# Expert weights as unconverted float32 in two column halves of TensorE, with four smaller moves ahead of them

## The chip, the cores and the metric

The kernel runs on 1 core of one Trainium2 chip. The metric is the device time of one execution in microseconds; lower is better. The engines are TensorE (PE, with its weight loads PEld), VectorE (DVE), ScalarE (ACT), GpSimd (POOL) and SyncE (SP), which here only issues DMAs.

## What is computed

One layer of a streaming encoder on 256 tokens of 1024 features, all in float32: three token mixers on the same input, gates, an output projection, a LayerNorm, then a mixture of 16 experts and a second LayerNorm. Cut to what matters (the routing takes one group of four experts for each token, and the best two inside it):

```python
proj = x @ w_in + b_in                        # 1024 -> 9216 columns
a = a_val * sigmoid(a_gate)                   # mixer A
a = causal_depthwise_conv(a, conv_a_w) + conv_a_b        # 31 taps
a = silu(layer_norm(a, ln_a_g, ln_a_b))
y_a = a @ w_a_out
y_b, y_c = ...                                # short convolution, pooling
mix = (g[0] * y_a + g[1] * y_b + g[2] * y_c) @ w_o + b_o
x = layer_norm(DEEPNORM_ALPHA * x + mix, ln1_g, ln1_b)
for e in range(16):                           # grouped_moe
    h = silu(x @ w_exp_gate[e]) * (x @ w_exp_up[e])      # 1024 -> 512
    y = y + combine[:, e:e + 1] * (h @ w_exp_down[e])    # 512 -> 1024
out = layer_norm(DEEPNORM_ALPHA * x + y, ln2_g, ln2_b)
```

The matrices are 152 MB in float32, each read once.

## The kernel before

**Chunks and slots.** The weights lie in memory as 145 chunks of 1 MB, 128 partitions by 2048 float32: 49 for the mixers (list `MIX`) and 96 for the experts (`EXP`), six for each expert `e`: two halves of the gate matrix (`EG`), two of the up matrix (`EU`), two of the down matrix (`ED`). `give` (L139) hands freed buffers back and issues the next chunk's load on SP whenever one of the slots of 1 MB is free, so that the loads run ahead of the work as far as the slots reach; `hold` keeps some slots back for other uses.

**Two parts for each weight.** A weight isn't multiplied as it is. ACT copies it into a rounded form, fp32r (`hi`, L163), and DVE or POOL forms the remainder (`lo`, L173); both lie in slots of their own (`H` and `L` in the rows, or other slots' names that were reused). The activations have two such parts too. A product is then three matmuls in fp32r in the mixers (L306 for chunk 0, L315 for the others, L518 for the last ones).

**Experts.** Each expert has 64 places for tokens (CAP). A gather (L836 for the first group of four experts, L944 for the others) brings the tokens' features into `XG`, transposed, the two parts side by side: a stationary tile of 128 columns, 64 with the rounded parts and 64 with the remainders. So `mm` (L980) needs two matmuls of 512 columns for each block of 128 features, one against `H` and one against `L`: 8 to a chunk, 32 for gate and up of one expert. The eviction `ev_gu` (L987, L989) adds the upper 64 rows onto the lower. `hidden` (L997) transposes the two results back, in eight blocks of 64 columns, and forms the hidden activations. For the down matrix, 80 of the 96 chunks of the experts being converted and 16 not, one half of `ED` is taken by `mm` again, and the other by `mm_native` (L1032) in plain float32 with a stationary tile of 64 columns; such a matmul stands in the trace as two instructions, each of them 512 columns. Then `scatter` (L1023, L1026) adds the expert's output, weighted, into four banks of PSUM (`acc`) that all experts share. A small matmul (L965) makes the matrices that scatter needs.

**What sets the order.** In the mixers a scheduler orders the engines' queues; `at(j, f)` ties a step to the work of chunk `j`, and `convert(j + 2)` runs two chunks ahead of the matmuls. The LayerNorm of mixer A hangs on one number, `LNA` = 34: its sums are matmuls with ones (L449 for the mean, L467 for the variance), with the squares added up by one reduction on DVE (L462) between them, and four blocks of swish for each of two chunks from `LNA + 4` on; the blocks' remainders are formed on POOL (L268). From the last mixer chunks on the order is the one that is written down (`tc.manual_schedule`), on each engine by itself. The transition between mixers and experts holds the first LayerNorm of the layer (`add1`, L642; `x1a`, L682), the logits and the softmax (L677), the choice of experts (`select`), and the comparison `places` (L820) whose result `ps` the gathers need; the conversion of the first three chunks of the experts is woven into it. The second LayerNorm (L1196 to L1220) and the stores end the kernel.

## Time and profile before

| | us |
|---|---|
| median of 3 runs | 612.66 (610.72 to 613.81) |
| profiled execution | 614.9 |
| its span in the trace | 613.1 |
| span up to the experts' first matmul | 317.3 |
| experts' stage up to the end of its last matmul | 281.5 |
| what is left to the end of the span | 14.3 |
| mean granted clock of TensorE | 0.979 of full speed |

The profiled execution is 1.8 us longer than its span, and 2.2 us longer than the median. In the rows below, L12 is line 12 of the kernel; `x` is a count of instructions; a buffer's number is left out of its name, and `128*64` is a TensorE tile of 128 rows and 64 columns. In brackets stands how long an engine was idle just ahead of the instruction, and what ended that.

### The profile page before, as it was taken

What the parts mean: (1) busy time and instruction counts of PE and PEld (TensorE: products, weight loads), DVE (VectorE), ACT (ScalarE), POOL (GpSimd) and SP (SyncE); (2) the same over time, 40 slices, a digit from 0 to 9 for tenths busy, and PEclk for the clock granted to TensorE, in tenths of its full rate; (3) what the DMA queues carried; (4) which work ended last, traced back from release to release, by engine and by line L of the source; (5) the groups of instructions that cost most, each with busy time, mean ns of one, the idle gap of its engine ahead of it and who ended that gap; (6) DMA issues with size and microseconds to landing.
All of it is one profiled execution on the core that took longest, in us unless ns stands there. A gap on an engine that the chain in (4) does not pass through costs nothing. (4 is left out here: it accounts for less than half of the span.)

```text
span 613.1 us, 9493 instructions
## 1 busy us (share of the span) xinstructions
PE 581.2 (95%) x3554; PEld 481.7 (79%) x3554; DVE 545.1 (89%) x862; ACT 373.8 (61%) x536; POOL 194.3 (32%) x150
## 2 busy tenths in 40 slices
PE   7999999999999998899999998999999999999990
PEld 5999999999999998798878466666566667666650
DVE  4899999999996578876889699899999999999985
ACT  5643544446643456745247496888678886888851
POOL 2876899987689420500000022000000000000003
PEclk9999999999999998899989997999999999999997
DMA  8985545455557645566479784899989998998102
GB/s 302 422 338 192 170 175 196 149 206 185 177 196 266 210 149 211 214 233 249 159 277 387 285 340 150 332 382 385 399 320 366 390 408 309 373 386 328 68 1 73
DMA packets 24084, 158.77 MB, mean 259 GB/s; under 512 B 2784, under 2 KB 3040, under 8 KB 5472
## 3 DMA queue, kind: packets, MB, share of 16 engines
q1 hardware_dynamic: 24032, 158.10, 68.4%
q8 instruction: 30, 0.49, 0.3%
q14 instruction: 22, 0.18, 0.1%
HBM read 157.04 MB, written 1.05 MB: 258 GB/s over the span
## 5 line engine op out<-in xcount | busy, mean ns | idle before, releaser
L315 PE MATMUL pj<-XH,H 128*128 128x256 f32 x560 | 138.7, 285 | 0.0
L315 PE MATMUL pj<-XL,H 128*128 128x256 f32 x560 | 138.3, 284 | 0.0
L163 ACT ACTIVATE H<-R 128x1024 fp32r<-128x1024 f32 (+1 forms) x74 | 72.2, 1027 | 67.2 <-issue 30.0
L315 PEld LDWEIGHTS pj<-XH,H 128*128 128x128 f32 x560 | 108.3, 193 | 0.1
L315 PEld LDWEIGHTS pj<-XL,H 128*128 128x128 f32 x560 | 108.3, 193 | 0.1
L337 DVE SCALAR_TENSOR_TENSOR z<-UP,par,z 128x256 f32<-128x256 f32 x232 | 98.8, 480 | 0.7
L173 POOL TENSOR_TENSOR L<-R,H 128x1024 fp32r<-128x1024 f32 (+2 forms) x50 | 88.0, 1783 | 21.2 <-ACT H L163 21.2
L320 PE MATMUL pj<-XH,L 128*128 128x256 f32 x560 | 78.6, 283 | 0.0
L1199 POOL TENSOR_TENSOR sm<-sm,mhalf 128x1 f32<-128x1 f32 x2 | 1.1, 551 | 228.3 <-DVE sm L1198 228.3
L173 DVE TENSOR_TENSOR L<-R,H 128x768 fp32r<-128x768 f32 (+2 forms) x46 | 62.7, 1378 | 11.5 <-ACT H L163 11.5
L320 PEld LDWEIGHTS pj<-XH,L 128*128 128x128 f32 x560 | 72.2, 192 | 0.0
L163 ACT ACTIVATE H<-S 128x1024 fp32r<-128x1024 f32 x30 | 30.1, 1050 | 29.2 <-issue 16.6
L173 POOL TENSOR_TENSOR L<-S,H 128x1024 fp32r<-128x1024 f32 (+1 forms) x20 | 36.6, 1855 | 1.1 <-ACT H L163 1.1
L987 ACT ACTIVATE t2k<-pj 64x512 f32<-64x512 f32 x32 | 19.1, 596 | 23.7 <-PE pj L980 21.5
L173 DVE TENSOR_TENSOR L<-S,H 128x768 fp32r<-128x768 f32 (+1 forms) x16 | 24.1, 1519 | 5.5 <-ACT H L163 5.4
L989 DVE TENSOR_TENSOR t2k<-pj,t2k 64x512 f32<-64x512 f32 x32 | 21.6, 676 | 3.8 <-ACT t2k L987 3.6
L268 POOL TENSOR_TENSOR R<-UP,YL 128x512 fp32r<-128x512 f32 x4 | 7.4, 1858 | 54.4 <-ACT YL L267 54.4
L1026 PEld LDWEIGHTS z<-t2k,pt 128*128 128x128 f32 x60 | 10.2, 188 | 11.2 <-ACT hs L1010 7.3
L1026 PE MATMUL z<-t2k,pt 128*128 128x512 f32 x60 | 17.7, 416 | 0.0
L944 PEld LDWEIGHTS pj<-ps,YL 128*128 128x128 f32 x48 | 8.8, 206 | 10.8 <-DVE ps L820 3.9
L268 POOL TENSOR_TENSOR AL<-t2k,AH 128x256 fp32r<-128x256 f32 x8 | 9.0, 1136 | 25.7 <-ACT AH L267 25.7
L944 PE MATMUL pj<-ps,YL 128*128 128x256 f32 x48 | 11.9, 321 | 5.2 <-DVE ps L820 4.7
(491 smaller groups left out, 1429.5 us busy)
## 6 DMA issues: line engine op xcount, KB each, us to landing
R<-w SPq DMA_DIRECT2D x51, 1024.0 KB, 5.0
S<-w SPq DMA_DIRECT2D x25, 1024.0 KB, 5.2
L<-w SPq DMA_DIRECT2D x11, 1024.0 KB, 7.4
H<-w SPq DMA_DIRECT2D x11, 1024.0 KB, 7.1
AC<-w SPq DMA_DIRECT2D x6, 1024.0 KB, 6.1
PL<-w SPq DMA_DIRECT2D x6, 1024.0 KB, 7.7
M<-w SPq DMA_DIRECT2D x6, 1024.0 KB, 7.8
XH<-w SPq DMA_DIRECT2D x6, 1024.0 KB, 7.9
```

Source lines behind the costliest of these rows:

```text
L163: S.activation(HI[j][:, o], raw[j][:, o], AF.Copy)
L173: eng.tensor_tensor(LO[j][:, o], raw[j][:, o], HI[j][:, o].bitcast(F32), op=OP.subtract)
L268: eng.tensor_tensor(dl, src, dh.bitcast(F32), op=OP.subtract)
L315: PE.matmul(p[:, c], h[:, o:o + 128], m[:, k0 + k], start=(n == 0), stop=False)
L320: PE.matmul(p[:, c], l[:, o:o + 128], ah[:, k0 + k], start=False, stop=(n == 3 * nk))
L337: V.scalar_tensor_tensor(AC[:, i] if k == TAPS - 1 else ca, src, wk, ca, op0=OP.mult, op1=OP.add)
L944: PE.matmul(p[:, n], xs[:, t, (4 * b + k) * 128:(4 * b + k + 1) * 128], PS[:, t, :, 0], start=(t == 0), stop=(t == 1))
L987: S.activation(t, p[64:], AF.Copy)
L989: V.tensor_tensor(GU[e, n], p[:64], t, op=OP.add)
L1026: PE.matmul(acc[t, b], PTs[e][:, t], YV[e, b][n], start=False, stop=(e == NE - 1 and n == 1))
L1199: G.tensor_tensor(mv[:, 2:3], mv[:, 1:2], mhalf, op=OP.pow)
```

## The change

It has five parts.

1. **Experts.** No chunk of an expert is converted. A weight chunk as it was loaded is the moving operand of a float32 matmul, and the stationary tile is 64 columns of unsplit tokens. `gate_up(e)` issues for each of eight blocks of 128 features two such matmuls, one with the gate's weights into the rows 0 to 63 of a PSUM bank and one with the up weights into the rows 64 to 127: the two stand in the two halves of TensorE's columns. `down(e)` does the same with the two halves of `ED`, four times two. There is one eviction of 128 rows on ACT, four transposes of 128 columns instead of eight of 64, and a scatter of eight matmuls for each expert, each with 64 rows of the contraction, in the two halves of the rows. The slots that held parts now hold chunks: 20 of them circulate, against some that were half as many chunks with their two parts. The expert's chunks come in the order gate, up, gate, up. The last two chunks of all, not the last one, are loaded in pieces of 512, and the last expert's `down`, its scatter and its statistics go in halves of 256 columns. The normalization at the end uses a PSUM bank between its two DVE steps, and each part is stored as soon as it is there.
2. **Chunk 0.** Its weights are laid out by feature blocks, its pieces and those of x are loaded in turn, and its matmuls go by pairs of feature blocks into two PSUM banks.
3. **LayerNorm of mixer A.** `LNA` is 31. The reduction of the squares is three additions instead, the matmul for the variance has one chunk more between itself and them, swish goes three blocks to a chunk, and its remainders are formed on DVE instead of POOL.
4. **Last mixer chunks.** For the last four of them the eviction of the chunk before (`done`) is put ahead of the conversion for the chunk after next.
5. **Transition.** The conversions of the experts' first three chunks are gone from it; the writing of a quarter of the LayerNorm (`x1a(1, 1)` and `x1b(1, 1)`, L682 and L686) goes behind `select` and `places`; matmuls whose result isn't used (`warm_up`) are 8 instead of 16; and the first gather's eviction is two copies, one on ACT and one on DVE.

The core of the diff (the loop over the experts, evictions and names that changed alike are left out):

```diff
-    def mm(p, lhs, j, first, last, mid=None):
-        h, l = HI[j], LO[j]
-        for n, ws in enumerate((h, l)):
-            if n and mid:
-                mid()
-            for k in range(4):
-                PE.matmul(p, lhs(k), ws[:, 512 * k:512 * k + 512],
-                          start=(first and n == 0 and k == 0), stop=(last and n == 1 and k == 3))
-        used(j)
+    def gate_up(e):
+        p = bank("pj", (128, 512))
+        for k in range(KT):
+            js = [INDEX[kind, e, k // 4] for kind in ("EG", "EU")]
+            for n, j in enumerate(js):
+                PE.matmul(p[64 * n:64 * n + 64], XG[e // 4][:, k, e % 4], raw[j][:, 512 * (k % 4):512 * (k % 4) + 512],
+                          start=(k == 0), stop=(k == KT - 1))
+            if k % 4 == 3:
+                for j in js:
+                    used(j)
+        g = GU[e] = t2k([128, 512])
+        S.activation(g, p, AF.Copy)
...
     def hidden(e):
-        p = bank("pj", (128, 2, 4, 64))
-        for n in range(2):
-            for k in range(4):
-                PE.transpose(p[:, n, k], GU[e, n][:, 128 * k:128 * k + 128], ident[:64, :64])
-        HS[e] = HSB
+        p = bank("pj", (128, 4, 2, 64))
+        for k in range(4):
+            PE.transpose(p[:, k], GU[e][:, 128 * k:128 * k + 128], ident)
...
+    def down(e, p, a=0, b=512):
+        js = [INDEX["ED", e, n] for n in range(2)]
+        for k in range(4):
+            for n, j in enumerate(js):
+                PE.matmul(p[64 * n:64 * n + 64], HF[e][:, k], raw[j][:, 512 * k + a:512 * k + b], start=(k == 0), stop=(k == 3))
+        if b == 512:
+            for j in js:
+                used(j)
...
-    def scatter(e, b):
+    def scatter(e, a=0, b=512):
         for t in range(2):
-            if b and e < NE - 1 or e == 0:
-                PE.matmul(acc[t, b], PTs[e][:, t], YV[e, b], start=False, stop=False)
-            else:
+            for i, y in enumerate(YV[e]):
                 for n in range(2):
-                    PE.matmul(acc[t, b], PTs[e][:, t], YV[e, b][n], start=False, stop=(e == NE - 1 and n == 1))
+                    r = slice(64 * n, 64 * n + 64)
+                    PE.matmul(acc[t, n][:, a:b], PTs[e][r, t], y[r, a:b], start=False,
+                              stop=(e == NE - 1 and i == 1), skip_group_check=(a > 0))
...
+    for e in range(NE):
+        while e // 2 not in ready:
+            some()
+        gate_up(e)
...
+        if e > 1:
+            scatter(e - 2)
...
+        last = e == NE - 1
+        if last:
+            hidden(e)
+        if e:
             p = bank("pj", (128, 512))
-            block(lambda j: mm(p, tokens(e, 0), j, True, False), before=last)
+            down(e - 1, p)
+            ev_down(e - 1, p)
+        if not last:
+            hidden(e)
...
             j = nxt[0]
             tags[j] = free.pop(-1 if dynamic[0] else 0)
             raw[j] = slot(tags[j], [128, 2048])
-            n = 512 if j == len(CHUNKS) - 1 else 2048
+            n = 512 if j >= len(CHUNKS) - 2 else 2048
             for i in range(0, 2048, n):
...
         h, l = HI[j], LO[j]
-            for c in range(js):
-                for b in range(2):
-                    for n, (ws, m) in enumerate(((h, ah), (h, al), (l, ah))):
-                        for k in range(4 * b, 4 * b + 4):
-                            o = (c * nk + k) * 128
-                            PE.matmul(p[:, c], ws[:, o:o + 128], m[:, k], start=(b == n == 0 and k == 0),
-                                      stop=(b == 1 and n == 2 and k == 7))
+            pp = [p[:, 0], bank()[:, 0]]
+            for b in range(4):
+                for n, (ws, m) in enumerate(((h, ah), (h, al), (l, ah))):
+                    for k in (2 * b, 2 * b + 1):
+                        for c in range(js):
+                            o = (k * js + c) * 128
+                            PE.matmul(pp[c], ws[:, o:o + 128], m[:, k], start=(b == n == 0 and k == 0),
+                                      stop=(b == 3 and n == 2 and k == 7))
...
-            V.tensor_reduce(sv, sq.rearrange("p i t -> p t i"), axis=AX.X, op=OP.add)
+            V.tensor_tensor(sq[:, :4], sq[:, :4], sq[:, 4:], op=OP.add)
+            V.tensor_tensor(sq[:, :2], sq[:, :2], sq[:, 2:4], op=OP.add)
+            V.tensor_tensor(sv, sq[:, 0], sq[:, 1], op=OP.add)
...
-            halves(A["h"][:, i], A["l"][:, i], z, G)
+            halves(A["h"][:, i], A["l"][:, i], z, V)
         at(j, center)
         at(j + 1, squares)
-        at(j + 1, var, True)
-        at(j + 2, rstd)
+        at(j + 2, var, True)
+        at(j + 3, rstd)
         for i in range(KT):
-            at(j + 2 + i // 4, lambda i=i: swish(i), True)
+            at(j + 3 + i // 3, lambda i=i: swish(i), True)
...
-    LNA = 34
+    LNA = 31
...
+        late = j > NM - 5
+        if done and late:
+            done()
+            done = None
         if j + 2 < NM:
             convert(j + 2, CUT if j < LNA else 0)
...
+                if a:
+                    V.tensor_copy(o, p[:, a:a + 2])
+                else:
+                    S.activation(o, p[:, a:a + 2], AF.Copy)
...
     x1a(0, 0)
     x1a(0, 1)
-    lo(C1, V, 0, 1024)
     logits(0, 0)
...
-    x1a(1, 1)
-    x1b(1, 0)
+    residual2(0, 0)
+    residual2(0, 1)
     u1 = shift1(1)
     softmax1(1, u1)
-    x1b(1, 1)
+    x1b(1, 0)
     S.activation(dummy, ex[1][:, :1], AF.Sigmoid)
-    warm_up(16)
+    warm_up(8)
     weave(best2(1), best_group(1))
     select(1)
+    x1a(1, 1)
     place1(1)
     warm_up(8)
     places(0, 1, 0, 2)
-    lo(C2, V, 0, 512)
+    x1b(1, 1)
...
-            V.scalar_tensor_tensor(u, z, mv[:, :1], g, op0=OP.subtract, op1=OP.mult)
-            V.scalar_tensor_tensor(u, u, mv[:, 2:3], c, op0=OP.mult, op1=OP.add)
-    def store(t, a, b, o):
-        nc.sync.dma_start(out[t * 128:t * 128 + 128, a:b], o[:, t, a:b])
+            v = bank("pj", (128, b - a))
+            V.scalar_tensor_tensor(v, z, mv[:, :1], g, op0=OP.subtract, op1=OP.mult)
+            V.scalar_tensor_tensor(u, v, mv[:, 2:3], c, op0=OP.mult, op1=OP.add)
```

In the rows below, a name with numbers is one use of a buffer, and line numbers are each kernel's own (L965 of after is `gate_up`, L988 `down`, L976 the transposes, L1007 the scatter).

On PE, the experts' steady work before: one expert's converted down half (against `hs`), the transposes (against `ident`), the native down half of the expert before (against `ssum`), the scatter (`z` is one bank of `acc`), and the next expert's gate.

```order
L980 MATMUL pj_4921<-H_647_4883,hs 128x512 x4
L980 MATMUL pj_4921<-M_4885,hs 128x512 x4
L997 MATMUL pj_4932<-ident,t2k_4881 128x64 x4
L997 MATMUL pj_4932<-ident,t2k_4913 128x64 x4
L1032 MATMUL pj_4958<-S_571_4572,ssum_4757 64x512 x4
L1026 MATMUL z_3628<-t2k_4943,pt_4720 128x512
L1026 MATMUL z_3628<-t2k_4944,pt_4720 128x512
L1026 MATMUL z_3626<-t2k_4943,pt_4720 128x512
L1026 MATMUL z_3626<-t2k_4944,pt_4720 128x512
L980 MATMUL pj_4967<-XL_4915,R_626_4776 128x512 x4
L980 MATMUL pj_4967<-S_655_4917,R_626_4776 128x512 x4
```

And on PE after, at the like place: the end of `down` of one expert, the transposes of the next, gate and up of the one after, in turn, and the beginning of a scatter, whose rows name two banks in turn.

```order
L988 MATMUL pj_4148<-R_413_3875,ssum_4085 64x512
L988 MATMUL pj_4148<-S_422_3902,ssum_4085 64x512
L976 MATMUL pj_4165<-ident,t2k_4124 128x128 x4
L965 MATMUL pj_4175<-AH_3904,XL_3934 64x512
L965 MATMUL pj_4175<-UP_3930,XL_3934 64x512
L965 MATMUL pj_4175<-AH_3904,XL_3934 64x512
L965 MATMUL pj_4175<-UP_3930,XL_3934 64x512
...
L965 MATMUL pj_4175<-PL_3954,XL_3934 64x512
L1007 MATMUL z_3620<-t2k_4161,pt_3889 128x512
L1007 MATMUL z_3621<-t2k_4161,pt_3889 128x512
L1007 MATMUL z_3620<-t2k_4162,pt_3889 128x512
L1007 MATMUL z_3621<-t2k_4162,pt_3889 128x512
```

The 8 rows of L980 for gate and up of one expert, of four matmuls each, are 16 single ones that alternate between two weight buffers.

On DVE, in the transition before, from the last evictions of the mixers (L642) to the second half's softmax (L677); L173 is the conversion of an expert's chunk, L682 half of the LayerNorm's writing, L820 `places`.

```order
L173 TENSOR_TENSOR H_334_3536<-R_286_3121,AH_3474 128x512 x2
L642 TENSOR_TENSOR UP_3107<-z_3280,UP_3107 128x256
...
L648 BN_STATS sm_3595<-UP_3107 128x6
L764 TENSOR_TENSOR sm_3652<-pj_3650,sm_3592 128x16
L653 BN_AGGR sm_3662<-sm_3595 128x2
L654 TENSOR_SCALAR sm_3662<-sm_3662 128x1
L682 SCALAR_TENSOR_TENSOR UP_3107<-UP_3107,sm_3662,PH_3111 128x512
L820 TENSOR_TENSOR ps<-sm_3652,slotn 128x256
L682 SCALAR_TENSOR_TENSOR UP_3107<-UP_3107,sm_3662,PH_3111 128x512
L686 SCALAR_TENSOR_TENSOR UP_3107<-UP_3107,sm_3663,PH_3111 128x512
L677 SCALAR_TENSOR_TENSOR sm_3692<-rs,sm_3662,pj_3659 128x16
```

After, at the same place.

```order
L648 BN_STATS sm_3587<-UP_3048 128x6 x2
L642 TENSOR_TENSOR UP_3048<-z_3285,UP_3048 128x256
L648 BN_STATS sm_3587<-UP_3048 128x6
L642 TENSOR_TENSOR UP_3048<-z_3285,UP_3048 128x256
L648 BN_STATS sm_3587<-UP_3048 128x6
L764 TENSOR_TENSOR sm_3644<-pj_3642,sm_3584 128x16
L653 BN_AGGR sm_3654<-sm_3587 128x2
L654 TENSOR_SCALAR sm_3654<-sm_3654 128x1
L682 SCALAR_TENSOR_TENSOR UP_3048<-UP_3048,sm_3654,PH_3052 128x512
L818 TENSOR_TENSOR ps<-sm_3644,slotn 128x256
L677 SCALAR_TENSOR_TENSOR sm_3683<-rs,sm_3654,pj_3651 128x16
```

L173 is gone from ahead of the second L642, and the second L682 stands further behind, after L677.

On DVE, around the LayerNorm of mixer A before: the square sums (L462) and the conversions (L173) beside them; L457 subtracts the mean.

```order
L173 TENSOR_TENSOR L_223_2608<-R_189_2129,H_222_2606 128x1024 x2
L173 TENSOR_TENSOR L_228_2669<-R_194_2199,H_227_2667 128x1024 x2
L173 TENSOR_TENSOR L_235_2732<-R_199_2272,H_234_2730 128x1024 x2
L457 TENSOR_TENSOR AC_170<-AC_170,t2k_2741 128x1024 x2
L443 TENSOR_TENSOR t2k_2804<-pj_2747,t2k_2675 128x512
L173 TENSOR_TENSOR L_241_2798<-R_204_2344,H_240_2796 128x1024 x2
L462 TENSOR_REDUCE t2k_2808<-PH_2729 128x256
L173 TENSOR_TENSOR L_248_2863<-S_209_2414,H_247_2861 128x1024
```

After: L459 to L461 are the three additions.

```order
L168 TENSOR_TENSOR L_214_2486<-S_181_1987,H_213_2484 128x1024 x2
L168 TENSOR_TENSOR L_221_2549<-R_185_2056,H_220_2547 128x1024 x2
L454 TENSOR_TENSOR AC_170<-AC_170,t2k_2558 128x1024 x2
L440 TENSOR_TENSOR t2k_2621<-pj_2564,t2k_2492 128x512
L168 TENSOR_TENSOR L_227_2615<-R_190_2130,H_226_2613 128x1024 x2
L459 TENSOR_TENSOR PH_2546<-PH_2546 128x1024
L460 TENSOR_TENSOR PH_2546<-PH_2546 128x512
L461 TENSOR_TENSOR t2k_2625<-PH_2546 128x256
L168 TENSOR_TENSOR L_233_2680<-R_195_2200,H_232_2678 128x1024 x2
```

The order of the steps stays, and the reduction is three instructions. On PE, the variance's matmul now has the matmuls of three chunks between itself and those for the mean, where it had two, and both stand three chunks and two chunks earlier.

## Rows read from the trace of the kernel before

**Rows 1.** The page's first part: busy us, share of the span and instructions of each engine.
```profile
PE 581.2 (95%) x3554; PEld 481.7 (79%) x3554; DVE 545.1 (89%) x862; ACT 373.8 (61%) x536; POOL 194.3 (32%) x150
```

**Rows 2.** Windows of 20 us: length, busy PE, PEld, DVE, ACT, POOL; granted clock; DMA share; GB/s.
```profile
20.00:40.00 20.00, 20.00 (x169) 20.00 (x168) 18.60 (x27) 10.49 (x13) 17.82 (x11) 1.00 1.02 415
220.00:240.00 20.00, 17.84 (x135) 17.46 (x134) 18.66 (x15) 9.34 (x12) 3.83 (x2) 0.91 0.60 211
240.00:260.00 20.00, 17.96 (x132) 17.10 (x130) 17.62 (x25) 16.34 (x30) 7.55 (x6) 0.91 0.48 168
360.00:380.00 20.00, 16.81 (x63) 11.22 (x63) 19.30 (x24) 13.82 (x23) 7.36 (x4) 0.83 0.67 264
480.00:500.00 20.00, 20.00 (x87) 13.95 (x86) 19.72 (x23) 15.86 (x22) 0.00 (x0) 1.00 0.99 388
```

**Rows 3.** The chain that ended last, inside the experts: start us, us, what.
```profile
476.37 3.72 PE pj L980 x16
480.09 0.46 PE z L1023 x2
...
484.45 2.10 PE pj L980 x8
486.55 0.64 PE pj L997 x8
487.19 3.58 PE pj L1032 x8
490.77 1.14 PE z L1026 x4
```

**Rows 4.** Timeline of PE: the experts' first and last matmuls; start us, us, instruction.
```profile
317.30 1.61 PE L980 MATMUL pj<-H,YH 128*128 128x512 f32 x4
...
597.72 1.09 PE L1026 MATMUL z<-t2k,pt 128*128 128x512 f32 x4
```

**Rows 5.** The waits, grouped: engine, line <- releaser: us, count, longest.
```profile
PE pj L944 <- DVE ps L820: 4.7, 5, 2.8
```

**Rows 6.** Timeline of PE and PEld at a plain float32 down half of 64 columns.
```profile
555.13 0.14 PEld L1032 LDWEIGHTS pj<-L,ssum 128*64 128x64 f32 x1 [0.29 <-issue]
555.56 0.14 PEld L1032 LDWEIGHTS pj<-L,ssum 128*64 128x64 f32 x1 [0.29 <-issue]
...
557.70 0.59 PE L1032 MATMUL pj<-L,ssum 128*64 128x512 f32 x1
558.23 1.21 PE L1026 MATMUL z<-t2k,pt 128*128 128x512 f32 x4
```

**Rows 7.** Groups by line and shape: ACT's conversions into one kind of slot.
```profile
L163 ACT ACTIVATE H<-R 128x1024 fp32r<-128x1024 f32 x70 | 70.0, 1050 | 65.4 <-issue 30.0 <-POOL L L173 22.0 <-PE pj L315 6.5
```

**Rows 8.** Timeline of DVE and PE around the LayerNorm of mixer A.
```profile
228.14 3.74 DVE L462 TENSOR_REDUCE t2k<-PH 128x256 f32<-128x2048 f32 x1
...
231.94 1.22 PE L467 MATMUL pj<-t2k,ones 128*128 128x256 f32 x2 [2.16 <-DVE t2k L462]
...
253.69 0.51 PE L315 MATMUL pj<-AH,H 128*128 128x256 f32 x2 [0.81 <-ACT AH L267]
255.41 0.51 PE L315 MATMUL pj<-AL,H 128*128 128x256 f32 x2 [1.22 <-POOL AL L268]
```

**Rows 9.** Timeline of DVE in the transition from the mixers to the experts.
```profile
305.38 1.28 DVE L173 TENSOR_TENSOR H<-R,AH 128x512 fp32r<-128x512 f32 x2
306.58 0.42 DVE L642 TENSOR_TENSOR UP<-z,UP 128x256 f32<-128x256 f32 x1
...
310.96 0.23 DVE L677 SCALAR_TENSOR_TENSOR sm<-rs,sm,pj 128x16 f32<-128x16 f32 x1
```

**Rows 10.** Timeline of PE at chunk 0 and at a late mixer chunk.
```profile
8.29 0.80 PE L306 MATMUL pj<-XH,H 128*128 128x256 f32 x2 [2.30 <-ACT XH L267]
...
288.92 0.73 PE L518 MATMUL z<-XH,YH 128*128 128x512 f32 x2 [0.60 <-ACT YH L267]
```

**Rows 11.** Timeline of DVE: the last step of the last LayerNorm.
```profile
606.69 0.42 DVE L1209 TENSOR_TENSOR M<-M,H 128x256 f32<-128x256 f32 x1
```

## What I predicted, and how it is worked out

> **What bounds the kernel now.** I read the busy times first: PE is busy for 581.2 of 613.1 us [rows 1], so time goes only where PE has less to do or waits less. Then the windows of 20 us, to see where it isn't full: in the first chunks and in the experts it is busy for 20.00 of 20 at clock 1.00, in the middle of the mixers there are two windows of 17.84 and 17.96 at 0.91, and one of 16.81 at 0.83 early in the experts [rows 2]. Then the chain that ended last: in the experts its pieces are PE's matmuls, end to end, and a steady expert takes 476.37 to 491.91, that is 15.54 us [rows 3]. So the experts' stage, from 317.30 to 597.72 + 1.09 = 598.81 [rows 4], 281.5 us, is a sum of matmuls. The waits come last [rows 5]: they show what could be had beside the matmuls.
>
> **Experts: what goes.** A piece of 16 matmuls of L980 takes 3.72 us [rows 3], 0.2325 each; there are 640, 40 to an expert: 148.8. The native halves: 16 of 3.58 = 57.3. Transposes: 16 of 0.64 = 10.2. Scatters: 16 of 0.46 and 15 of 1.14 [rows 3] = 24.5, and about 1.7 for the last expert's, an estimate from four of the 0.46's halves at float32's double time. Together 242.5 of 281.5. The 39.0 that remain are gathers, residual sums, small matmuls for the scatter, and waits. Their counts stay. Of the waits, 4.7 us are the gathers', for the comparison on DVE [rows 5]; it is now queued a block sooner, on an engine that loses the conversions. With the clock's dip beside it (0.83 for 20 us is 3.4 us lost [rows 2], which began with those waits) I take 5 of some 8 off: 34 stay; none or all of it is 39 or 31.
>
> **Experts: what comes.** A float32 matmul against 64 columns is two instructions, and a native half has 8 of them in 3.58 us [rows 3], 0.4475 each, so 0.895 for a matmul. Now gate and up are 16 such matmuls and down 8, each in one half of the columns, the partner right behind it in the other half. If partners run side by side, a pair costs what one does: 12 x 0.895 = 10.74 for an expert, 171.8 for 16. If not, 343.7. No row before has two matmuls in different halves of the columns; the two ends are this term's bounds. I take the first. What speaks for it: a float32 instruction of 512 columns takes 0.4475 and one of fp32r 0.2325 [rows 3], each with 512 x 4 bytes to a row, so two float32 streams at once read 2 x 512 x 4 bytes in 0.4475 us, a rate only 4% above that of one fp32r stream now.
>
> Transposes are four in place of eight; I take 0.5 of the 0.64 us (0.32 to 0.64 are the bounds): 8.0. The scatter is eight matmuls of 512 columns, in two halves of the rows: at 1.14 / 4 = 0.285 a pair [rows 3] 1.14 for an expert, 18.2; one after the other it is twice that, 36.5. Sum added: 171.8 + 8.0 + 18.2 = 198. The stage becomes 34 + 198 = 232, **-49.5**. Evictions: one ACT copy of 512 columns follows `gate_up`, and the transposes come only after `down` of the expert before, 3.6 us later; `down` needs the hidden activations only after the next `gate_up`, 7.2 us later. With the conversions gone (one piece of 1024 columns is 1.05 us on ACT [rows 7]) neither ACT nor DVE is near PE.
>
> **Loads.** What the experts need, 96 chunks, PE would now use up at 14.5 us for six. 22 are issued before the first expert frees a slot, 74 remain. At 415 GB/s, or at 388 in the experts [rows 2], a chunk of 1.05 MB takes 2.53 or 2.70 us: 187 or 200 us, under the 232. Loads decide only under 74 x 1.05 / 230 = 336 GB/s. That is why I cost them at nothing; the cover is 30 us.
>
> **Mixers.** The variance matmul waited 2.16 us for a reduction of 3.74 us, and the product after the LayerNorm 0.81 for ACT's part and 1.22 for POOL's [rows 8]: 4.2 together. The two windows at 0.91 lose 1.8 us each [rows 2], 3.6; they lie right at the waits. With one more block of cover (about 5 us of matmuls), the additions in place of the reduction, and the remainders on DVE, I expect the waits gone and half of the clock's loss: **-6**, bounds -3.8 (clock stays) and -7.8 (all). If the wait is not gone it is DVE's, whose queue now holds the remainders behind conversions.
>
> Chunk 0: PE waits 2.30 us for ACT's part of x [rows 10]; pieces in turn and pairs of features let it start with a quarter of both. PE then is bound by the pieces' arrival: **-1**, between +0.5 and -2.5. Evictions ahead of the conversions: a wait of 0.60 [rows 10], **-0.3**, 0 to -0.6. Transition: the conversion of 1.28 us stands right ahead of the last additions on DVE [rows 9], on the path PE waits for: 1.3; the step of LayerNorm's writing ahead of the softmax 1.2 (of the 310.96 - 306.58 = 4.4 between them); the first gather's evictions 0.3: **-2.8**, bounds -1.2 and -3.5. End: DVE's last step ends at 606.69 + 0.42 [rows 11]; POOL takes a part of it and a store follows each piece: **-0.5**, 0 to -1.5. Together -10.6.
>
> **Sum.** -49.5 - 10.6 = -60.1 on the profiled execution of 614.9: 554.8. That execution stands 2.2 over the median of 612.66, so the forecast is **552.6 us**. The small terms' bounds add up to about -4.5 and -16; with the 31 to 39, full overlap spans 543 to 564.
>
> **Rivals.** *Halves one after the other.* Then 171.8 us more: 552.6 + 171.8 = 724, and 743 if the scatter's halves do so too. That is slower by 18%. The mechanism is in the pair: the second matmul of 0.895 begins when the first ends. Break-even: the whole saving of 60.1 is gone when 35% of 171.8 isn't had, thus when a pair takes over 1.21 us instead of 0.895 (192 x 0.313 = 60.1). For it: no row shows an overlap. Against it: the bytes above, and that half the columns stand idle in L1032.
>
> *Loads of weights in the open.* A load of 64 columns takes 0.14 us, and follows the one before at 0.43 us [rows 6], so in one half it is hidden under the matmul. If the four loads of a pair were all in the open, 192 x 4 x 0.14 = 107.5 us more: 660. The Trainium skill, "TensorE: Matmul & The Clock Gate", Part 3, in its passage on packing small matmuls, speaks for this: it says that a load overlaps a matmul of another row group, and both halves here use all rows. The rows above speak against it: L1032's loads lie under matmuls of the same rows.
>
> *Overlap in part.* Each eighth of the second matmul's 0.895 that doesn't overlap is 192 x 0.112 = 21.5 us: 574 at one eighth, 596 at a quarter. For it: the streams ask a little more than one does now; against: no row shows two of them. The same passage of the Trainium skill gives three column tiles 2.38 times the speed of one, 0.79 of the full gain; at that the pair would be 0.895 / 0.79 = 1.13, an estimate from that page, and no run here shows it.
>
> *Loads bind.* At 300 GB/s the 74 chunks take 259 us: 28 more, 580. For it: 264 GB/s in a window of the experts [rows 2]; against: that window was slot-bound, with DMA share 0.67, and 0.99 shows 388.
>
> *Switches of the tile shape.* From the native half to the scatter PE's rows go 557.70 to 558.23, 0.53 where 0.43 is usual, and four scatter matmuls take 1.14 instead of 4 x 0.2325 = 0.93 [rows 3, 6]: some 0.3 us for such a change, which the block prices above contain. After has five to an expert where before had three: 16 x 2 x 0.3 = 10 us if none of it is in these prices: 562, inside the range. The Trainium skill, "TensorEngine Tiling (Array Packing)", Key Properties, says that a change of tiling mode drains TensorE; it agrees.
>
> **How the numbers follow.** Full overlap (540 to 565): 0.62. In part (565 to 600): 0.15. One after the other (about 724 to 743): 0.12. Loads in the open (about 660): 0.05. Bound by DMA (about 580): 0.04. Something unseen, to either side: 0.02. The range takes the first, second and fifth, 536 to 600: 0.81. Within 0.5% is about what a measurement can tell from no change; between 600 and 660 lies little, so 0.02 for the same; faster 0.82, slower 0.16.
>
> **What would show it.** `gate_up`: 16 program matmuls in some 7.2 us, `down` 3.6, a steady expert about 14.5 us where it was 15.54; records of two halves that overlap. PE still full in the experts, DMA share under 1 there, no conversions on ACT and DVE, the stage 232 us long. In the mixers: the waits of 2.16, 0.81 and 1.22 gone and the clock nearer 1.00; the experts' first matmul at about 307 instead of 317.3. It is wrong if a pair takes over 1.0 us, or if PE waits for chunks.

## The result

| | before | after |
|---|---|---|
| median, us | 612.95 (610.72 to 613.81) | 542.53 (542.26 to 543.10) |
| profiled execution | 614.9 | 543.1 |
| span | 613.1 | 541.3 |
| span up to the experts' first matmul | 317.3 | 306.0 |
| experts' stage | 281.5 | 220.9 |
| what is left | 14.3 | 14.5 |

The changed kernel takes 0.886 of the time, interval 0.883 to 0.888. The forecast was 552.6, its range 536 to 600: direction and place are right, and 10 us more were gained than forecast, nearly all of them in the experts' stage. The measured time lies just under the 543 to 564 us that the forecast's own bounds gave for full overlap; it is inside the stated range by the slack that was left below them.

The busy times after, as in [rows 1]:

```profile
PE 520.9 (96%) x3538; PEld 382.9 (71%) x3538; DVE 317.1 (59%) x626; ACT 191.3 (35%) x301; POOL 169.2 (31%) x134
```

PE is still what bounds the kernel; VectorE went from 89% to 59%. The windows of 20 us that [rows 2] show, with the same columns:

```profile
20.00:40.00 20.00, 20.00 (x169) 20.00 (x169) 19.57 (x30) 11.37 (x14) 19.02 (x11) 1.00 1.02 419
...
220.00:240.00 20.00, 20.00 (x169) 20.00 (x168) 18.43 (x26) 13.47 (x23) 3.02 (x2) 1.00 0.46 158
240.00:260.00 20.00, 20.00 (x162) 19.69 (x161) 17.40 (x30) 12.32 (x19) 0.00 (x0) 1.00 0.89 336
...
480.00:500.00 20.00, 20.00 (x100) 7.37 (x98) 3.34 (x8) 3.18 (x7) 0.00 (x0) 1.00 1.01 421
```

In the mixers PE is full at clock 1.00 where it was at 17.84, 17.96 and 0.91. In the experts VectorE and ScalarE are nearly idle, and the loads run at a DMA share of 1.01 and 421 GB/s, where the forecast went by the 388 of the window that it showed.

The chain that ended last, in one expert (start us, us, what), to be read beside [rows 3]. L965 is `gate_up`, L1007 the scatter, L953 the small matmuls for it, L988 `down`, L976 the transposes:

```profile
434.56 1.13 PE z L1007 x8
435.69 0.61 PE pj L953 x4
436.30 3.58 PE pj L988 x16
439.88 0.59 PE pj L976 x4
440.47 7.02 PE pj L965 x32
```

16 instructions of `down` take 3.58 us where 8 did, and 32 of `gate_up` take 7.02. The timeline of PE at the first expert shows how (start us, us, instruction):

```profile
305.96 0.64 PE L965 MATMUL pj<-R,YH 128*64 128x512 f32 x1
305.97 0.64 PE L965 MATMUL pj<-XH,YH 128*64 128x512 f32 x1
306.44 0.59 PE L965 MATMUL pj<-R,YH 128*64 128x512 f32 x1
306.45 0.59 PE L965 MATMUL pj<-XH,YH 128*64 128x512 f32 x1
```

Two instructions on different weight buffers start 0.01 us apart. The next two follow 0.48 us later, and from then on it is 0.43. The two halves run side by side all the way.

### The profile page after: what moved, and what is told of

Same layout as the page of the kernel before. It is cut to its first block, busy times and chain, and to the rows that moved or that the text cites. A ratio compares the mean times of both kernels' runs of the same rounds, so it can differ in the third digit from the quotient of the medians.

```text
span 541.3 us, 8851 instructions
## 1 busy us (share of the span) xinstructions
PE 520.9 (96%) x3538; PEld 382.9 (71%) x3538; DVE 317.1 (59%) x626; ACT 191.3 (35%) x301; POOL 169.2 (31%) x134
## 4 chain that ended last, share of the span: by engine, by line
PE 92%; DVE 2%; DMA 1%; POOL 1%; SPq 1%; issue 0%; ACT 0%; POOLq 0%
PE pj L311 30%; PE pj L965 21%; PE pj L316 15%; PE pj L988 11%; PE z L517 4%; PE z L1007 3%; PE pj L937 2%; PE pj L976 2%; DMA R<-w 1%; PE pj L837 1%; PE pj L418 1%; PE pj L953 1%; PE z L809 1%; POOL L L168 1%; SPq L211 0%
## 5 line engine op out<-in xcount | busy, mean ns | idle before, releaser
L158 ACT ACTIVATE H<-R 128x1024 fp32r<-128x1024 f32 (+1 forms) x70 | 68.2, 1025 | 63.7 <-issue 29.1
L168 POOL TENSOR_TENSOR L<-R,H 128x1024 fp32r<-128x1024 f32 (+2 forms) x48 | 84.2, 1778 | 18.6 <-ACT H L158 18.6
L999 DVE SCALAR_TENSOR_TENSOR t2k<-pj,cw,t2k 128x512 fp32r<-128x512 f32 (+1 forms) x17 | 12.2, 719 | 108.5 <-ACT t2k L998 108.5
L971 ACT ACTIVATE t2k<-pj 128x512 f32<-128x512 f32 x16 | 9.6, 598 | 109.3 <-PE pj L965 109.3
L158 ACT ACTIVATE H<-S 128x1024 fp32r<-128x1024 f32 x28 | 28.1, 1050 | 25.7 <-issue 14.3
L168 POOL TENSOR_TENSOR L<-S,H 128x1024 fp32r<-128x1024 f32 (+1 forms) x16 | 29.8, 1880 | 1.1 <-ACT H L158 1.1
L998 ACT ACTIVATE t2k<-pj,cw 128x512 fp32r<-128x512 f32 (+1 forms) x17 | 11.3, 664 | 52.3 <-PE pj L988 52.3
L168 DVE TENSOR_TENSOR L<-S,H 128x1024 fp32r<-128x1024 f32 (+1 forms) x20 | 27.4, 1378 | 2.2 <-ACT H L158 2.1
L965 PE MATMUL pj<-R,YH 128*64 128x512 f32 x64 | 24.9, 596 | 0.0
L988 PE MATMUL pj<-L,ssum 128*64 128x512 f32 (+1 forms) x56 | 21.9, 537 | 0.0
L1007 PEld LDWEIGHTS z<-t2k,pt 64*128 64x128 f32 x136 | 11.4, 184 | 14.6 <-issue 11.7
```

Of the source, the lines that this page charges most:

```text
L158: S.activation(HI[j][:, o], raw[j][:, o], AF.Copy)
L168: eng.tensor_tensor(LO[j][:, o], raw[j][:, o], HI[j][:, o].bitcast(F32), op=OP.subtract)
L965: PE.matmul(p[64 * n:64 * n + 64], XG[e // 4][:, k, e % 4], raw[j][:, 512 * (k % 4):512 * (k % 4) + 512], start=(k == 0), stop=(k == KT - 1))
L988: PE.matmul(p[64 * n:64 * n + 64], HF[e][:, k], raw[j][:, 512 * k + a:512 * k + b], start=(k == 0), stop=(k == 3))
L998: S.activation(yh, p, AF.Copy, scale=CW[e])
L999: V.scalar_tensor_tensor(yl, p, CW[e], yh.bitcast(F32), op0=OP.mult, op1=OP.subtract)
```

## The experiments

There were twelve runs, one of them the changed kernel again. Times are compared with the changed kernel: 542.53, and 542.78 (542.41 to 542.92) when it was timed again. One column half, four and four, a quarter of the conversions and no scatters were executed once each, the others five times. Four of the mixers' runs (the LayerNorm undone, chunk 0, the transition, the evictions) were on another chip, where the kernel before took 611.8 us and not 612.9 as beside the changed kernel timed again; a difference under about 1 us isn't settled there.

### Do the halves carry it?

First, gate and up into the same column half:

```diff
-        p = bank("pj", (128, 512))
+        ps = [bank("pj", (64, 512)) for n in range(2)]
...
-                PE.matmul(p[64 * n:64 * n + 64], XG[e // 4][:, k, e % 4], raw[j][:, 512 * (k % 4):512 * (k % 4) + 512],
+                PE.matmul(ps[n], XG[e // 4][:, k, e % 4], raw[j][:, 512 * (k % 4):512 * (k % 4) + 512],
...
-        S.activation(g, p, AF.Copy)
+        for n in range(2):
+            S.activation(g[64 * n:64 * n + 64], ps[n], AF.Copy)
```

> Only change against the changed kernel: gate and up of an expert go to the same column half (two PSUM banks of 64 rows, two ACT copies of 64 rows instead of one of 128); same matmuls in the same order. Theory (the gain of the float32 matmuls is that the two column halves run side by side): a pair of gate_up takes 2 x 0.855 us instead of 0.855, 16 x 8 x 0.855 = 109 us more, about 652 us. Rival (a float32 matmul of 64 columns is spaced by 0.43 us for each instruction pair in any place, the halves don't matter): no change, 543 us.

652.3 us. The theory's number to 0.5 us; the rival falls. The chain of this kernel, `gate_up` (L965) and `down` (L989, still in two halves):

```profile
442.73 3.58 PE pj L989 x16
...
447.84 13.88 PE pj L965 x32
```

13.88 against 7.02 is 6.86 us for an expert, 109.8 for 16. A pair in two halves takes what one of its matmuls takes alone, 0.86 us (6.86 / 8 here).

### Must the halves alternate?

Then the order: four matmuls to one half, then four to the other.

```diff
-        for k in range(KT):
-            js = [INDEX[kind, e, k // 4] for kind in ("EG", "EU")]
+        for b in range(2):
+            js = [INDEX[kind, e, b] for kind in ("EG", "EU")]
             for n, j in enumerate(js):
+                for k in range(4 * b, 4 * b + 4):
...
-        for k in range(4):
-            for n, j in enumerate(js):
+        for n, j in enumerate(js):
+            for k in range(4):
                 PE.matmul(p[64 * n:64 * n + 64], HF[e][:, k],
```

> Only change: the matmuls of the two column halves don't alternate, four go to one half and then four to the other, in gate_up and in down. Theory (TensorE starts matmuls in the order of its queue, and a matmul overlaps only the one queued right ahead of it, if that is in the other half): overlap remains only at the ends of the blocks of four. If the overlap there is a whole matmul of 0.855, gate_up is 13 units instead of 8 and down 7 instead of 4: 16 x 8 x 0.855 = 109 us more, 652 us; if it is one of a matmul's two instructions, 14.5 and 7.5 units: 137 us more, 680 us. Rival A (TensorE finds the free half's work further back in its queue): 543 to 560 us. Rival B (no overlap at all is left): 164 us more, 707 us.

601.1 us, 58.5 more: none of the four numbers. The order costs, but about half of the least that the theory said (109 us). Chain (L988 `down`, L966 `gate_up`), and the timeline of one `down`, in which `L` and `H` hold the two halves' weights:

```profile
435.73 5.35 PE pj L988 x16
441.08 0.59 PE pj L976 x4
...
442.61 8.90 PE pj L966 x32
```

```profile
417.61 2.36 PE L988 MATMUL pj<-L,ssum 128*64 128x512 f32 x5
419.38 0.64 PE L988 MATMUL pj<-H,ssum 128*64 128x512 f32 x1
419.81 0.59 PE L988 MATMUL pj<-L,ssum 128*64 128x512 f32 x1
419.86 0.59 PE L988 MATMUL pj<-H,ssum 128*64 128x512 f32 x1
```

The eight instructions on `L` begin at 417.61 and follow at 0.43. All of them stand ahead of those on `H` in the queue, but the first on `H` starts at 419.38, at the same time as the fifth on `L` and ahead of the last three. So four instructions of each half, that is two matmuls, overlap at each change of half. The working agrees with the times: `down` 16 - 4 = 12 places of 0.43 are 5.1 us, with the 0.16 that a block has beside its places (3.58 less 8 of 0.4275) 5.3 (5.35); `gate_up` 32 - 3 x 4 = 20 places are 8.6 (8.90). That reading was made after the run, so the next run tested it, with two matmuls to a half (the same edit with `range(2 * b, 2 * b + 2)`, four blocks in `gate_up`, two in `down`).

> Two matmuls to one column half, then two to the other, in gate_up and down. In the run with four and four, the other half's first instruction began when four instructions of the first half were still to come (itself at the same time as the fourth last). Theory (an instruction for the free half starts while up to four of the other half stand ahead of it, which is two matmuls): the overlap stays whole but for the first two matmuls of a block, at most 16 x 2 x 0.855 = 27 us more if each block's ends count, and 0 to 5 us if only the first pair of gate_up and of down is late by 0.1; I take within 5 us, 543 to 548. Rival (each change of the half costs a fixed share): the four-and-four order has 6 changes to an expert and costs 58.5 us over 16, 0.61 us each; two and two has 10 changes: 98 us more, 640 us.

543.99 us (543.98 to 544.35), 1.2 more than the changed kernel beside it; the theory holds. The rival's 640 is out, and it would be further out had it counted the changes of half in the four-and-four order rightly: they are four to an expert, three in `gate_up` and one in `down`, not six. The chain:

```profile
436.71 3.63 PE pj L990 x16
440.35 0.59 PE pj L977 x4
440.93 7.07 PE pj L966 x32
```

That is 0.05 us more for each `down` and each `gate_up`. Alternation one by one isn't needed: two float32 matmuls to a half in turn cost next to nothing, four cost 58.5 us, and three were not run.

### Where did the other 10 us come from?

The kernel before, with a quarter of its conversions in the experts:

```diff
-                PE.matmul(p, lhs(k), ws[:, 512 * k:512 * k + 512],
+                PE.matmul(p, lhs(k), ws[:, :512],
...
-            convert(CONV[n], 0, 512 if n + 4 >= len(CONV) else 1024, m)
+            if CONV[n] in raw:
+                left.setdefault(CONV[n], 512)
+                hi(CONV[n], 256 * m, 256 * m + 256)
+                lo(CONV[n], V, 256 * m, 256 * m + 256)
```

> The kernel before, with a quarter of the conversions of the experts' chunks from the fourth on: only columns 0 to 511 of a chunk are converted, and all four blocks of features are multiplied with these (the products are thus other ones); matmuls, loads and slots stay as they were. Theory (in the experts' stage before, some 18 us of TensorE's 281.5 us were waits, mostly short ones for conversions on VectorE that its busy time hides): the stage falls by 10 to 16 us, to about 598 to 603 us. Rival A (the waits were for loads and for the comparison that gathers need): at most 4 us, 609 us or more. Rival B (there were no such waits, and what the change gained beyond the forecast came from cheaper matmuls): 613 us.

595.5 us, where the kernel before took 610.4 on the same chip. The timeline's first and last matmuls of the experts:

```profile
313.58 1.61 PE L980 MATMUL pj<-H,YH 128*128 128x512 f32 x4
...
578.32 1.09 PE L1026 MATMUL z<-t2k,pt 128*128 128x512 f32 x4
```

The stage is 265.8 us instead of 281.5: 15.7 less with the same 1160 matmul records, at the upper end of the theory's 10 to 16. Both rivals fall. (The total, 595.5, is under the theory's 598 to 603, which was reckoned from 613 to 614 us for the kernel before; on this chip that took 610.4.) The stage as one window, before and in this run, with the columns of [rows 2]:

```profile
317.30:598.81 281.51, 273.34 (x1160) 183.80 (x1160) 263.17 (x352) 213.24 (x305) 7.36 (x4) 0.99 0.78 306
```

```profile
313.58:579.41 265.83, 265.68 (x1160) 182.67 (x1160) 142.18 (x342) 116.78 (x297) 5.85 (x4) 1.00 0.82 324
```

Of the 15.7 us, 8.0 were idle time of PE that the profile shows (8.2 before, 0.15 here), and 3.4 are the clock of the one window at 0.83 [rows 2], which is at 1.00 here. The other 4 or so lie in the busy time of the same matmuls; I take them for waits too short to show beside the modelled ends of the matmuls, and that is not shown by itself. The number is also one execution against another, and the kernel before varies between 610 and 615.

Conversions also free slots for loads. No run changes that part alone, but the profile of before puts none of the waits in the stage, on any engine, down to a transfer. Its chain speaks for the conversions: there the chain of the experts leaves PE, again and again, for them (start us, us, what; L173 is the remainder on VectorE, L163 the rounding on ScalarE, L820 the comparison for the gathers):

```profile
467.38 0.59 DVE t2k L989
467.97 2.28 DVE UP L173 x2
470.25 0.04 issue
470.29 0.73 PE pj L980 x2
...
501.19 0.96 ACT XL L163
502.14 0.02 issue
502.16 2.36 DVE XH L173 x2
504.52 1.22 DVE ps L820 x2
505.74 0.04 issue
505.78 0.62 PE pj L944 x3
```

### How much cover have the loads now?

The changed kernel without the scatters of experts 0 to 13:

```diff
-        if e > 1:
-            scatter(e - 2)
```

> The changed kernel without the scatter matmuls of experts 0 to 13 (their outputs are left out): 14 x 1.13 = 15.8 us less on TensorE. Theory (loads run at their limit of 421 GB/s through the experts, and the last chunk lands only some 10 us before it is needed): about 10 us less, 533 us, with TensorE waiting for chunks at the end. Rival (loads have the cover of 30 us of the prediction): 15.8 us less, 527 us.

530.2 us: 12.3 less, of 15.8 taken from PE, between the theory's 10 and the rival's 15.8. Its timeline and its last full window:

```profile
497.62 0.64 PE L965 MATMUL pj<-PL,XL 128*64 128x512 f32 x1 [1.14 <-DMA PL<-w]
```

```profile
480.00:500.00 20.00, 18.86 (x88) 7.39 (x87) 3.01 (x6) 2.52 (x5) 0.00 (x0) 1.00 1.01 421
```

PE waits for a chunk, as the theory had it, and isn't full at the end. Not all of the 3.5 us that were not gained are the loads': 0.7 of them is a wait of the last transposes for ScalarE's eviction, which a scatter had covered. So the cover is some 12 us, and far from the forecast's 30.

### The mixers' parts, one undone at a time

All of the LayerNorm's part undone (the `-` and `+` of the diff above exchanged, from `LNA` to `halves`):

```diff
-    LNA = 31
+    LNA = 34
```

> The changed kernel with the LayerNorm of mixer A as before (LNA 34, one reduction, variance after two chunks, swish by four, remainders on GpSimd). Theory (the waits of 4.2 us and part of the clock's loss come back): 6 us more, between 3.8 and 7.8, 546 to 550 us, with waits of about 2, 0.8 and 1.2 us at the variance's matmul and at the product after it. Rival (with the conversions for the experts gone from behind, the mixers' stage hides them): within 1 us.

551.7 us (550.8 to 552.5): 9.0 more. The waits of PE (engine, line <- releaser: us, count, longest) and the window where they fall:

```profile
PE pj L464 <- DVE t2k L459: 2.1, 1, 2.1
...
PE pj L311 <- POOL AL L263: 1.2, 1, 1.2
...
PE pj L311 <- ACT AH L262: 0.8, 1, 0.8
```

```profile
240.00:260.00 20.00, 17.93 (x118) 16.80 (x117) 13.99 (x22) 12.62 (x26) 8.03 (x8) 0.83 0.75 289
```

The same three waits as in [rows 8], 4.1 us, and a window at a granted clock of 0.83, 3.4 us: 7.5. The remaining 1.5 have no row that I found. The window with the first of the waits, however, is at full clock, where it was at 0.91 before [rows 2]:

```profile
220.00:240.00 20.00, 17.85 (x147) 17.60 (x147) 18.91 (x15) 11.93 (x14) 2.75 (x2) 1.00 0.58 211
```

Then `LNA` stays at 31, and all the rest of the LayerNorm's part is as before; beside these lines the reduction and GpSimd's remainders come back too:

```diff
-        at(j + 2, var, True)
-        at(j + 3, rstd)
+        at(j + 1, var, True)
+        at(j + 2, rstd)
...
-            at(j + 3 + i // 3, lambda i=i: swish(i), True)
+            at(j + 2 + i // 4, lambda i=i: swish(i), True)
```

> The changed kernel with the reduction, the two-chunk distance, swish by four and the remainders on GpSimd as before, and only LNA at 31: of the LayerNorm's part only the place in the row of chunks stays changed. Theory (most of the gain is the two kinds of wait, with the clock behind them, and the place takes away only the wait at the product after it): the variance's wait of about 2 us and its share of the clock come back, 3 to 5 us more than the changed kernel, 546 to 547 us. Rival A (the place is all that matters): within 1 us of it. Rival B (the place gives nothing): as with all of it undone, 9 us more, 552 us.

546.5 us (544.6 to 546.6): 3.7 more, as the theory had it. Its waits and its window:

```profile
PE pj L464 <- DVE t2k L459: 2.2, 1, 2.2
```

```profile
200.00:220.00 20.00, 17.84 (x135) 17.46 (x134) 19.43 (x16) 9.54 (x14) 4.03 (x2) 0.91 0.59 209
```

One wait of 2.2 and one window at 0.91, 1.8 us: 4.0, and the waits at the product after the LayerNorm are gone. So of the 9 us some 5 are the place's, and some 4 go with what this run puts back. Of that, the wait is the variance's; whether the additions or the longer distance end it, no run separates.

The other three:

```diff
-    START = tuple((m, i) for i in range(4) for m in "xw")
+    START = (("x", 0), ("w", 0), ("x", 1), ("x", 2), ("w", 1), ("x", 3), ("w", 2), ("w", 3))
```

(with the layout and the loops of chunk 0 as before)

> The changed kernel with chunk 0 laid out, loaded and multiplied as before. Theory: 1 us more, between 0.5 less and 2.5 more, 543.5 us. Rival (what TensorE waits for at the start is the arrival of the last pieces, in either order): no change.

543.84 us (542.5 to 544.7), 1.1 more, but the five runs reach from the changed kernel's time to 2 us over it. Not settled; it isn't more than 2. The traces show no gain: at chunk 0 PE waits three times here, 1.7 us together, and 2.0 us in the changed kernel.

```diff
-    x1a(1, 1)
     place1(1)
     warm_up(8)
     places(0, 1, 0, 2)
-    x1b(1, 1)
```

(both ahead of the softmax, `warm_up(16)`, and `residual2(0, .)` behind the first gate and up)

> The changed kernel with the writing of the second half's LayerNorm ahead of the softmax again, 16 instead of 8 unused matmuls, and two residual sums behind the first expert's gate and up instead of ahead; the conversions stay gone. Theory: 1.2 us for the LayerNorm's writing and up to 0.4 for the matmuls, 1.5 us more, 544 us. Rival (the whole gain in the transition was that of the conversions): no change.

544.3 us (543.9 to 544.7): 1.5 more than the changed kernel timed again, as the theory had it. The trace has a wait of PE that the changed kernel's doesn't have, at the matmul behind `select`:

```profile
PE pj L762 <- DVE sm L748: 1.1, 1, 1.1
```

```diff
-        late = j > NM - 5
+        late = False
```

> The changed kernel with the evictions of the last four mixer chunks behind the conversions again. Theory: 0.3 us more, between 0 and 0.6, 542.8 us, with a wait of TensorE of 0.6 us for a part of the merged activations at the last mixer chunks. Rival: no change.

543.2 us (542.9 to 543.3): 0.4 to 0.7 more, which is too little to tell from nothing across two chips. The wait of 0.6 that the theory expected isn't in the trace: the last mixer chunks' waits are the changed kernel's, 0.4 and 0.3, and the experts begin at 305.96 in both.

### The changed kernel again, and the end

> The changed kernel unaltered, timed beside the next three on one chip: 542.5 us, between 542 and 544, by both theories. It is what the single parts are compared with.

542.78 us. And with the stores in another order:

```diff
-        norm2(acc[t, a // 512][:, a % 512:a % 512 + b - a], mv2[t], t, a, b, eng, o2)
+        norm2(acc[t, a // 512][:, a % 512:a % 512 + b - a], mv2[t], t, a, b, eng, o2, False)
+    for t, a, b in ((0, 0, 512), (1, 0, 512), (0, 512, 1024), (1, 512, 768), (1, 768, 1024)):
+        nc.sync.dma_start(out[t * 128:t * 128 + 128, a:b], o2[:, t, a:b])
```

> The changed kernel with the five stores at the end queued in the order in which their parts are ready (VectorE's two halves first, then GpSimd's), where in the changed kernel the first in SyncE's queue is GpSimd's, ready at about 532.6 us while VectorE's first part is ready at 530.7. Theory (the last store starts about a microsecond sooner): 0.5 to 1.2 us less, about 541.7 us. Rival (the last store waits for GpSimd's last part in any order): no change.

541.87 us (541.0 to 542.5), 0.9 less. The ranges touch, so the time alone doesn't prove it; the traces agree with it. In the changed kernel VectorE's first part is ready at 529.91 + 0.75, GpSimd's at 531.33 + 1.27, and all stores stand behind that one (start us, us, instruction; SPq is SyncE's queue):

```profile
529.91 0.75 DVE L1104 SCALAR_TENSOR_TENSOR H<-pj,sm,AL 128x512 f32<-128x512 f32 x1
...
531.33 1.27 POOL L1099 TENSOR_TENSOR H<-H,AL 128x512 f32<-128x512 f32 x1
...
532.63 2.80 SPq L1106 DMA_DIRECT2D out<-H  x5
```

With the other order they are issued as the parts come:

```profile
530.13 3.74 SPq L1117 DMA_DIRECT2D out<-H  x5
```

## Why the prediction came out so, by its own steps

**What comes (198 us).** Right. The chain's share by line over the stage is 112.3 us for `gate_up`, 57.3 for `down`, 18.0 for the scatter and 9.3 for the transposes: 196.9. Taking the pair at one matmul's price was right, and the first experiment shows that it is the halves that do it. The argument from bytes (two float32 streams read little more than one of fp32r) led to the right end of a range of 172 us. The rival of loads in the open is out: 0.14 us for each of four loads would have made a pair 1.4 us, and it took 0.86. The Trainium skill, "TensorE: Matmul & The Clock Gate", Part 3, gives 2.38 for three column tiles; here two tiles gave 2.0, and the deduction from that figure, a pair of 1.13, doesn't hold for two.

**What goes (242.5 us) and what stays (34).** The mechanism was right here, and what stays was mis-sized: 24.0 us stayed, 10 less than the 34 and below the bound of 31. By counts and durations the gathers, small matmuls and residual sums are 22.7 us in the chain of after (12.5, 4.7, 3.7 and 1.9), and their counts are those of before, except that four of the eight residual matmuls now stand ahead of the stage. In the chain of the run with a quarter of the conversions the same kinds are 22.8 us. So of the 39.0 that I set down as remaining, some 16 were waits and lost clock, where I counted some 8 and took off 5. Two readings were wrong. I read one expert without a gather [rows 3], found PE's pieces end to end, and took it for all 16. And I wrote that PE is busy for 20.00 of 20 in the experts: of the 14 windows between 320 and 600 only six reach 19.9, and over the stage the profile shows 8.2 us of idle PE, of which the wait that I priced is 4.7. With a quarter of the conversions 15.7 us were gone. The row that should have told me is the chain beyond the piece that I quoted, with L173 in it time after time.

**Mixers and transition (-10.1).** -11.3 by the first matmul of the experts, 317.30 to 305.96. The LayerNorm was mis-sized: 9.0, over its bound of 7.8. I gave half of the clock's loss back, and all of it came back: the windows show 1.00. One more window of before, in the transition, lost 1.8 us of clock, for which I had no term; after, it is at 1.00:

```profile
300.00:320.00 20.00, 19.12 (x136) 16.89 (x136) 16.48 (x59) 7.98 (x16) 0.99 (x1) 0.91 0.55 211
```

For chunk 0, the evictions and the transition I had 4.1 and the profile leaves 2.7 if the LayerNorm's shift in the trace (314.62 to 305.96, 8.7) is taken off; undone one by one they sum to some 3, of which only the transition's 1.5 have a row in the traces. These don't include the conversions in the transition, which no run took back alone, nor the 1.7 us of residual sums that now stand ahead of the experts' first matmul.

**End (-0.5).** +0.2. Faster pieces, but the store queued first is that of the slowest engine.

**Loads.** Right that they don't bind, wrong in the cover. I compared 74 chunks' time with the stage as if all of it were open to them. The last chunk has landed by about 510 (45 GB/s from 510 to 512), 9 us before its matmuls, and the run without scatters shows 12. A stage of 221 instead of 232 took the rest.

**Tile shapes.** `down` takes 0.16 more than its eight places of 0.4275, and the sum of the blocks, changes included, came out at 196.9 of 198: no 10 us came on top.

## What to carry to other kernels

A float32 matmul with a stationary tile of 64 columns leaves half of TensorE's columns idle; a second one into the other half cost nothing here, and it made the splitting of weights on two other engines needless, which gave 15 us of the stage's 60.6 beside the 45.6 of the matmuls themselves. When an engine's work is removed, don't take its waits from the busy share of the engine that waits: subtract counts times durations from the stage, and what is left over is waits until a row says otherwise. After such a gain, look at once at the next bound; here the loads are 12 us away.

## What the runs showed of the hardware that I had not expected

TensorE began work in a free column half while four instructions of the other half, queued ahead of it, were starting or still to come (419.38 us, four and four); two matmuls to a half in turn cost 0.05 us for a block, and four to a half 1.8 us.

The loads ran at 421 GB/s and a DMA share of 1.01 from 340 to 500 us. That VectorE and ScalarE had nearly nothing to do is not the reason as far as the windows show: from 20 to 40 us the changed kernel's loads run at 419 with VectorE busy for 19.57 of 20, and in the experts' stage of before one window shows 414:

```profile
420.00:440.00 20.00, 18.92 (x77) 11.71 (x75) 19.41 (x26) 14.77 (x22) 0.00 (x0) 1.00 1.00 414
```

The same wait of 2.2 us of TensorE at the variance's matmul cost clock in two traces and none in two. In the kernel before (220 to 240) and with the place alone changed (200 to 220) its window is at 0.91, 1.8 us more; with all of the LayerNorm undone and in the run with a quarter of the conversions (both 220 to 240) it is at 1.00. What a wait costs in clock can't be read off its length.
